# A hybrid decoder trunk on one core: the low part of every second weight unit from an accumulating DMA

## The chip, the core and the metric

The kernel runs on one core of one Trainium2 chip. The metric is the device time of one execution in microseconds (us), the median of several runs; lower is better. TensorE (PE) does the matmuls and loads their stationary operand (PEld), VectorE (DVE), ScalarE (ACT) and GpSimd (POOL) do the elementwise work, and SyncE (SP), ACT and POOL can issue DMAs.

## The reference

Two layers over a sequence of 512 tokens and a width of 1024, everything in float32. Cut to what is computed:

```python
def hybrid_layer(x, ...):
    h = rmsnorm(x, norm_g)
    proj = h @ w_in                      # 1024 -> 9216 columns, split into the names below
    (rq, rk, rv, rz, sq, sk, sv, sz, cu, cz, ga, gb, gc) = split(proj)
    y_a = retention(rq, rk, rv, ...) * silu(rz)
    y_b = stick_breaking(sq, sk, sv, ...) * silu(sz)
    y_c = s5_ssm(cu, ..., w_glu, b_glu) * silu(cz)
    merged = sigmoid(ga) * (y_a @ proj_a) + sigmoid(gb) * (y_b @ proj_b) + sigmoid(gc) * (y_c @ proj_c)
    return x + merged @ w_out
```

Most of the arithmetic is the products with `w_in`, `w_glu`, `proj_a`, `proj_b`, `proj_c` and `w_out`.

## The kernel before

**Split products.** PE multiplies in float32r, a float32 operand that is rounded. To keep the precision, each operand of a large product is held as two float32r tiles: a high part (the rounded value) and a low part (the value minus its high part). The helper `three` then issues three matmuls for each block: high times high, high times low, low times high.

**Units.** The host cuts all large weights of a layer into 98 units of 128 x 1024 floats (512 KB), so there are 196 in all, in the order in which PE consumes them. The text `ORDER_TEXT` gives that order by item: `sk sq sv sz gb cu cz pb gc rq rk rv0 rv1 glu ga pc rz pa out0 out1`, with parts of some items interleaved. There are two kinds of items. A token-major item (`sk sq sv cu rq rk rv0 rv1 out0 out1`) takes four units at once. It goes through four token blocks ("pieces"), each of which reads all four units one after the other, and only after the fourth piece are the units free. A channel-major item takes one unit (or half a unit) per piece and frees it right after.

**Buffers.** Raw weights, high parts and low parts share one pool `wp` of 12 buffers. The class `Weights` runs it: `load` issues the DMA of a raw unit on SP, `make` turns the oldest raw unit into a pair (`wh` by an ACT copy, `wl` by a DVE subtraction), `take` hands a pair to PE, and `fill` makes up to four pairs ahead and keeps up to four raw units loaded. After the last piece of a token-major item `W.free` rises by four and `fill` makes the four units of the next item in one go; this is called a seam below. A buffer is reused as soon as the pool hands it out again, and the new writer waits for the last reader of the old tile: ACT's next `wh` for PE's last matmul on an old pair, a raw load for the DVE subtraction or the matmul that read the buffer before.

**Order.** Instructions stand on each engine in the order in which the program writes them. One main loop goes over the pieces; in each step come background generators that are due, then the piece's matmuls, then `W.fill()`. Background work (evacuations of a piece, normalisation, attention, retention chunks, the state space model) is written as generators that yield to later steps. Another background chain, which prepares coefficients on POOL and DVE, advances when counters of the estimated load of POOL and DVE are low enough; the counters are kept by the wrappers `TT`, `TS`, `STT`, `GT`, `GS` and `MM` (all recorded under line 197).

Names used below: `raw`, `wh`, `wl` are the three tiles of a unit; `mm` is the PSUM tile of a piece; `hh`, `hl` the halves of the normalised input; `mgh`, `mgl` those of the merged branches; `yah`, `yal` those of the retention branch. A matmul `mm<-wl,hh` has the low weights as moving operand (token-major), `mm<-hh,wl` as stationary operand (channel-major).

Of the kernel before, what the change touches and what calls it, by code (L numbers as in the profile page):

```python
# [10 lines left out]
F32 = mybir.dt.float32  # L11
F32R = mybir.dt.float32r
BF16 = mybir.dt.bfloat16
AF = mybir.ActivationFunctionType
ALU = mybir.AluOpType
PSUM = bass.MemoryType.PSUM

P = 128
# [168 lines left out]
def trunk(ctx: ExitStack, tc, x_in, w_in, par_in, bc_in, ng_in, cst_in, rope_in, out):  # L187
    nc = tc.nc
    load = {"V": 0.0, "G": 0.0, "T": 0.0}

    def counted(f, engine, each):


        def g(*a, **k):
            o = k["out"] if "out" in k else a[0]
            load[engine] += 0.07 * (engine != "T") + each * math.prod(o.shape[1:])
            return f(*a, **k)  # L197

        return g

    TT = counted(nc.vector.tensor_tensor, "V", 1.04e-3)
# [3 lines left out]
    ACT = nc.scalar.activation  # L205
# [3 lines left out]
    wp = ctx.enter_context(tc.tile_pool(name="wp", bufs=W_TILES))  # L209
# [31 lines left out]
    def C(n):  # L241
# [7 lines left out]
        out=negm, in_=negm, pattern=[[1, P]], base=0, channel_multiplier=-1, compare_op=ALU.is_ge, fill=0.0  # L249
# [45 lines left out]
    class Weights:  # L295
# [16 lines left out]
        def make(self):  # L312
            if not self.raw:
                self.load()
            raw = self.raw[0]
            wh = wp.tile([P, 1024], F32R, tag="w", name="wh")
            wl = wp.tile([P, 1024], F32R, tag="w", name="wl")
            ACT(wh, raw, AF.Copy)  # L318
            TT(out=wl, in0=raw, in1=wh.bitcast(F32), op=ALU.subtract)
            self.units.append((wh, wl))  # L320
            self.raw.pop(0)
            self.made += 1
# [1069 lines left out]
```

## Time and profile before

| | |
|---|---|
| median of 2 runs | 1311.69 us (1311.26 to 1312.12) |
| profiled execution | 1311.17 us, span 1309.5 us |
| PE busy | 1271.7 us, 97% |
| PEld busy | 1048.5 us, 80% |
| DVE busy | 855.6 us, 65% |
| ACT busy | 537.6 us, 41% |
| POOL busy | 382.5 us, 29% |
| mean granted clock of PE | 0.992 |

The span runs from the first to the last instruction of the profiled execution, and the time of that execution contains 1.7 us around it. Busy times are sums of instruction durations on an engine; they overlap with each other. A wait is an idle time of an engine that a semaphore ended, put down to the instruction that gave it. The granted clock is 1.00 at 2.4 GHz and 0.50 at 1.2 GHz.

### The profile page before, as it was taken

What the parts mean: (1) busy time and instruction counts of PE and PEld (TensorE: products, weight loads), DVE (VectorE), ACT (ScalarE), POOL (GpSimd) and SP (SyncE); (2) the same over time, 40 slices, a digit from 0 to 9 for tenths busy, and PEclk for the clock granted to TensorE, in tenths of its full rate; (3) what the DMA queues carried; (4) which work ended last, traced back from release to release, by engine and by line L of the source; (5) the groups of instructions that cost most, each with busy time, mean ns of one, the idle gap of its engine ahead of it and who ended that gap; (6) DMA issues with size and microseconds to landing.
All of it is one profiled execution on the core that took longest, in us unless ns stands there. A gap on an engine that the chain in (4) does not pass through costs nothing. (4 is left out here: it accounts for less than half of the span.)

```text
span 1309.5 us, 16640 instructions
## 1 busy us (share of the span) xinstructions
PE 1271.7 (97%) x6360; PEld 1048.5 (80%) x6360; DVE 855.6 (65%) x1189; ACT 537.6 (41%) x919; POOL 382.5 (29%) x452
## 2 busy tenths in 40 slices
PE   6989989999999999999999999899999999999998
PEld 5867768788887888888888877788888878888887
DVE  5997678776785438556365576789657844575542
ACT  5445534445343534332244445344534534423311
POOL 3340036638442012000042000584555311210000
PEclk9989989999999999999999999899999999999999
DMA  6232221222322322234433222122241232222342
GB/s 223 90 124 77 65 65 49 81 81 89 119 68 65 104 77 77 81 97 141 161 118 127 81 65 71 43 81 65 84 127 65 65 120 90 65 74 88 97 135 75
DMA packets 37375, 120.05 MB, mean 92 GB/s; under 512 B 4144, under 2 KB 4528, under 8 KB 37296
## 3 DMA queue, kind: packets, MB, share of 16 engines
q1 hardware_dynamic: 29664, 105.40, 25.2%
q10 hardware_dynamic: 7632, 13.59, 3.1%
q8 instruction: 50, 0.82, 0.3%
q14 instruction: 29, 0.24, 0.1%
HBM read 114.78 MB, written 4.19 MB: 91 GB/s over the span
## 5 line engine op out<-in xcount | busy, mean ns | idle before, releaser
L197 DVE TENSOR_TENSOR wl<-raw,wh 128x1024 fp32r<-128x1024 f32 x196 | 251.6, 1294 | 114.6 <-ACT wh L318 111.8
L197 PE MATMUL mm<-hh,wh 128*128 128x512 f32 x640 | 256.0, 400 | 0.0
L197 PE MATMUL mm<-hh,wl 128*128 128x512 f32 x640 | 251.2, 393 | 4.9 <-DVE wl L197 4.9
L197 PE MATMUL mm<-hl,wh 128*128 128x512 f32 x640 | 250.7, 392 | 0.0
L318 ACT ACTIVATE wh<-raw 128x1024 fp32r<-128x1024 f32 x196 | 205.8, 1057 | 86.7 <-PE mm L197 38.9
L197 PE MATMUL mm<-wh,hh 128*128 128x512 f32 x512 | 207.5, 405 | 0.9 <-ACT hh L421 0.9
L197 PE MATMUL mm<-wl,hh 128*128 128x512 f32 x512 | 202.6, 396 | 4.3 <-DVE wl L197 4.3
L197 PE MATMUL mm<-wh,hl 128*128 128x512 f32 x512 | 202.0, 395 | 0.0
L197 PEld LDWEIGHTS mm<-hh,wl 128*128 128x128 f32 x640 | 120.8, 189 | 32.2 <-DVE wl L197 6.3
L197 PEld LDWEIGHTS mm<-hh,wh 128*128 128x128 f32 x640 | 121.0, 189 | 25.1 <-issue 1.6
L197 PEld LDWEIGHTS mm<-hl,wh 128*128 128x128 f32 x640 | 121.0, 189 | 23.5
L197 PEld LDWEIGHTS mm<-wl,hh 128*128 128x128 f32 x512 | 104.5, 204 | 24.5 <-DVE wl L197 7.8
L197 PEld LDWEIGHTS mm<-wh,hh 128*128 128x128 f32 x512 | 104.5, 204 | 19.0 <-ACT hh L421 1.3
L197 PEld LDWEIGHTS mm<-wh,hl 128*128 128x128 f32 x512 | 104.2, 204 | 18.4 <-DVE hl L197 0.3
L1051 DVE TENSOR_TENSOR_SCAN kp<-kp,zero 128x511 f32<-128x511 f32 (+1 forms) x64 | 67.6, 1076 | 26.2 <-ACT kp L1047 26.1
L994 ACT ACTIVATE gate<-mm 128x512 f32<-128x512 f32 x48 | 28.6, 596 | 114.2 <-PE mm L197 114.2
L197 POOL TENSOR_SCALAR ms<-ss 128x8 f32<-128x8 f32 (+3 forms) x56 | 19.1, 341 | 181.5 <-DVE ss L824 100.6
L197 POOL TENSOR_TENSOR rs<-ms,mhalf 128x8 f32<-128x8 f32 (+3 forms) x56 | 64.6, 1154 | 4.7
L1033 POOL CAST qd<-qd 64x512 fp32r<-64x512 f32 x16 | 16.3, 1016 | 134.1 <-ACT qd L1028 133.7
L822 ACT ACTIVATE sq<-mm 128x512 f32<-128x512 f32 x32 | 19.0, 593 | 84.6 <-PE mm L197 84.5
L197 PE MATMUL mm<-wl,mgh 128*128 128x512 f32 x128 | 50.1, 391 | 0.2
L197 PE MATMUL mm<-wh,mgh 128*128 128x512 f32 x128 | 49.9, 390 | 0.0
(253 smaller groups left out, 2263.2 us busy)
## 6 DMA issues: line engine op xcount, KB each, us to landing
raw<-in_w SPq DMA_DIRECT2D x196, 512.0 KB, 3.5
x<-in_x SPq DMA_DIRECT2D x8, 256.0 KB, 7.3
rope<-in_rope ACTq DMA_DIRECT2D x8, 256.0 KB, 3.7
xh<-in_x ACTq DMA_DIRECT2D x8, 256.0 KB, 4.4
x<-xh ACTq DMA_DIRECT2D x8, 256.0 KB, 2.0
xh<-x ACTq DMA_DIRECT2D x8, 256.0 KB, 4.6
out<-xh ACTq DMA_DIRECT2D x8, 256.0 KB, 2.1
gB<-in_ng SPq DMA_DIRECT2D x2, 256.0 KB, 5.8
```

Of the source, the lines that this page charges most:

```text
L197: return f(*a, **k)
L318: ACT(wh, raw, AF.Copy)
L822: ACT(s2, ps, AF.Square)
L994: ACT(sg, ps, AF.Sigmoid)
L1033: nc.gpsimd.tensor_copy(out=qd[h][o, :], in_=qd[h][r, :])
L1051: nc.vector.tensor_tensor_scan(v, v, zero1.to_broadcast([P, n - 1]), 1.0, ALU.mult, ALU.add)
```

## The change

From unit 9 on, every second unit (9, 11, ..., 195; 94 of 196) gets its low part in another way. ACT writes the negated high part into a tile `wn` (a copy of the raw weights with scale -1, rounded like `wh`). Then POOL issues a DMA from `raw` to `wn` that adds to what is there, so that `wn` ends as raw minus high. The DVE subtraction of these units goes. The other units are made as before.

```diff
             raw = self.raw[0]
             wh = wp.tile([P, 1024], F32R, tag="w", name="wh")
-            wl = wp.tile([P, 1024], F32R, tag="w", name="wl")
             ACT(wh, raw, AF.Copy)
-            TT(out=wl, in0=raw, in1=wh.bitcast(F32), op=ALU.subtract)
+            if self.made % 2 and self.made > 7:
+
+                wn = wp.tile([P, 1024], F32R, tag="w", name="wn")
+                ACT(wn, raw, AF.Copy, scale=-1.0)
+                nc.gpsimd.dma_start(out=wn, in_=raw, accum_op=ALU.add)
+                wl = wn
+            else:
+                wl = wp.tile([P, 1024], F32R, tag="w", name="wl")
+                TT(out=wl, in0=raw, in1=wh.bitcast(F32), op=ALU.subtract)
             self.units.append((wh, wl))
             self.raw.pop(0)
             self.made += 1
```

All token-major items begin at an even unit, so in each of them the second and the fourth unit are of the new kind. Lines of the changed kernel behind this place have numbers higher by 7.

Three places in the order of instructions follow, all at the seam from `out1` of layer 0 to `sk` of layer 1 (units 98 to 101). The waits in brackets name semaphores: those of engines, DMAHW for DMAs that SP or ACT issue, DMASW for those that POOL issues.

ACT at that seam, before: four high parts (`wh`) in a row, then the store and the squares of the last block of `out1`.

```order
L421 ACTIVATE hh_82<-T4_5721 128x4x128 [waits PE_49]
L318 ACTIVATE wh_5755<-raw_5585 128x1024 [waits DMAHW4_49,PE_49]
L318 ACTIVATE wh_5761<-raw_5591 128x1024 [waits DMAHW5_49,PE_49]
L318 ACTIVATE wh_5767<-raw_5597 128x1024 [waits DMAHW6_49,DVE_49]
L318 ACTIVATE wh_5773<-raw_5603 128x1024 [waits DMAHW7_49,DVE_49]
L1264 DMA x1_87<-xh_5524 128x512 [waits DMAHW0_49,DVE_49]
L404 ACTIVATE xn_5781,ss_5607<-xh_5524 128x512
```

The same place on ACT in the changed kernel, with the negated copies (`wn`) of the second and the fourth unit.

```order
L428 ACTIVATE hh_82<-T4_5766 128x4x128 [waits PE_49]
L317 ACTIVATE wh_5800<-raw_5628 128x1024 [waits DMAHW4_49,PE_49]
L317 ACTIVATE wh_5806<-raw_5635 128x1024 [waits DMAHW5_49,PE_49]
L321 ACTIVATE wn_5808<-raw_5635 128x1024 [waits DMASW2_49,PE_49]
L317 ACTIVATE wh_5813<-raw_5641 128x1024 [waits DMAHW6_49,DVE_49]
L317 ACTIVATE wh_5819<-raw_5648 128x1024 [waits DMAHW0_49,DVE_49]
L321 ACTIVATE wn_5821<-raw_5648 128x1024 [waits DMASW5_49]
L1271 DMA x1_87<-xh_5567 128x512 [waits DMAHW7_49,DVE_49]
L411 ACTIVATE xn_5828,ss_5652<-xh_5567 128x512
```

The second negated copy waits for DMASW5, which is the accumulating DMA of the second unit, and the store and the squares stand behind it.

POOL at the same seam in the changed kernel: the two DMA issues stand between the statistics (`ss`, `ms`, `rs`) of the last two blocks of `out1`, which stood next to each other before.

```order
L197 TENSOR_TENSOR ss_5596<-ss_5596 128x1 [waits Activation_49]
L197 TENSOR_SCALAR ms_5756<-ss_5596 128x1 [waits Pool_49]
L197 TENSOR_TENSOR rs_5754<-ms_5756,mhalf_84 128x1 [waits Pool_49]
L322 DMA wn_5808<-raw_5635 128x1024 [waits DMASW2_49,DMAHW5_49,DVE_49,Activation_49]
L322 DMA wn_5821<-raw_5648 128x1024 [waits DMASW7_49,DMAHW0_49,DMASW5_49,Activation_49]
L197 TENSOR_TENSOR ss_5652<-ss_5652 128x1 [waits Activation_49]
L197 TENSOR_SCALAR ms_5832<-ss_5652 128x1 [waits DVE_49,Pool_49]
```

The second issue waits for the first one's landing too, through ACT and by a wait of its own; the statistics of the last block follow behind it.

## Rows read from the trace of the kernel before

**Rows 1.** The page, parts 1 and 2: busy time per engine, granted clock in 40 slices.
```profile
PE 1271.7 (97%) x6360; PEld 1048.5 (80%) x6360; DVE 855.6 (65%) x1189; ACT 537.6 (41%) x919; POOL 382.5 (29%) x452
...
PEclk9989989999999999999999999899999999999999
```

**Rows 2.** PE's own waits: instruction, releaser, us in total, times, longest.
```profile
PE wt L1068 <- DVE w L197: 13.5, 8, 3.1
PE mm L197 <- DVE wl L197: 9.2, 7, 3.3
```

**Rows 3.** Timeline at a pa unit of layer 1 (unit 181): start us, duration us.
```profile
1209.14 1.04 ACT L318 ACTIVATE wh<-raw 128x1024 fp32r<-128x1024 f32 x1
...
1223.94 0.39 PE L197 MATMUL mm<-yah,wl 128*128 128x512 f32 x1
```

**Rows 4.** Timeline at the seam to sk of layer 1 (units 98 to 101).
```profile
660.90 2.02 ACT L318 ACTIVATE wh<-raw 128x1024 fp32r<-128x1024 f32 x2
663.25 2.19 ACT L318 ACTIVATE wh<-raw 128x1024 fp32r<-128x1024 f32 x2 [0.33 <-DVE wl L197]
...
666.86 0.39 PE L197 MATMUL mm<-wl,hh 128*128 128x512 f32 x1
...
669.58 0.39 PE L197 MATMUL mm<-wl,hh 128*128 128x512 f32 x1
```

**Rows 5.** The page, part 5: busy us, mean ns of one, idle before.
```profile
L197 DVE TENSOR_TENSOR wl<-raw,wh 128x1024 fp32r<-128x1024 f32 x196 | 251.6, 1294 | 114.6 <-ACT wh L318 111.8
...
L318 ACT ACTIVATE wh<-raw 128x1024 fp32r<-128x1024 f32 x196 | 205.8, 1057 | 86.7 <-PE mm L197 38.9
```

**Rows 6.** The page, parts 3 and 6: the load queue, and the unit loads' landing.
```profile
q1 hardware_dynamic: 29664, 105.40, 25.2%
...
raw<-in_w SPq DMA_DIRECT2D x196, 512.0 KB, 3.5
```

**Rows 7.** POOL's short operations: the page's group, and timelines of POOL and DVE.
```profile
L197 POOL TENSOR_TENSOR rs<-ms,mhalf 128x8 f32<-128x8 f32 (+3 forms) x56 | 64.6, 1154 | 4.7
...
14.06 0.19 POOL L197 TENSOR_SCALAR ms<-ss 128x1 f32<-128x1 f32 x1
...
18.51 1.05 POOL L197 TENSOR_SCALAR ms<-ss 128x1 f32<-128x1 f32 x1
...
17.15 2.35 DVE L197 TENSOR_TENSOR wl<-raw,wh 128x1024 fp32r<-128x1024 f32 x2
```

**Rows 8.** The four unit loads between 655 and 672 us: from issue to landing.
```profile
DMA to landing us min/median/max: 3.5/5.2/5.4
```

**Rows 9.** Timelines at the seams to sv of layer 0 and out1 of layer 1.
```profile
61.17 1.06 ACT L318 ACTIVATE wh<-raw 128x1024 fp32r<-128x1024 f32 x1 [0.55 <-PE mm L197]
...
65.75 0.40 PE L197 MATMUL mm<-wl,hh 128*128 128x512 f32 x1
...
1281.02 2.96 ACT L318 ACTIVATE wh<-raw 128x1024 fp32r<-128x1024 f32 x3 [0.36 <-PE mm L197]
...
1285.29 0.39 PE L197 MATMUL mm<-wl,mgh 128*128 128x512 f32 x1
```

**Rows 10.** Timelines at the fourth unit of out0 and the fourth of rq, layer 0.
```profile
621.70 1.04 ACT L318 ACTIVATE wh<-raw 128x1024 fp32r<-128x1024 f32 x1
...
624.06 0.50 PE L197 MATMUL mm<-wl,mgh 128*128 128x512 f32 x1
...
330.73 1.06 ACT L318 ACTIVATE wh<-raw 128x1024 fp32r<-128x1024 f32 x1 [0.27 <-ACT gate L994]
...
336.51 0.39 PE L197 MATMUL mm<-wl,hh 128*128 128x512 f32 x1
```

**Rows 11.** Busy time by stretch; behind POOL's come granted clock, DMA share and GB/s.
```profile
92.50:97.60 5.10, 5.10 (x12) 4.03 (x13) 3.94 (x4) 4.58 (x6) 0.85 (x2) 0.50 0.07 6
188.40:193.20 4.80, 4.80 (x16) 4.24 (x17) 4.61 (x5) 0.98 (x2) 1.26 (x2) 0.50 0.23 67
410.00:417.00 7.00, 6.44 (x29) 5.03 (x30) 5.65 (x5) 2.64 (x5) 1.00 (x1) 1.00 0.38 119
```

## The prediction

> **What bounds the kernel now.** The page's busy line and its clock line come first: TensorE (PE) is busy 1271.7 of 1309.5 us and the granted clock stands near full speed throughout [rows 1]. The list of PE's own waits comes next. Only two entries matter after the start: 13.5 us in 8 waits of the attention transposes for VectorE (DVE), and 9.2 us in 7 waits of projection matmuls for a low part that DVE had not finished [rows 2]. So a change that only relieves DVE can win at most 13.5 + 9.2 = 22.7 us, and a few microseconds of clock. A change that makes a weight half arrive later is paid by PE in full as soon as the lead is used up. The question is therefore how much lead the low parts have, and where.
>
> The lead is read unit by unit, from the end of a unit's high-part copy on ScalarE (ACT) to the first matmul that reads its low part. Where units are consumed one at a time (the channel-major items) it is long, as with the 13.8 us of a pa unit in layer 1 (1223.94 - 1210.18) [rows 3]. Where one token-major item follows another it is short. In the sk item of layer 1, the high parts of the four units run at 660.90 and 663.25 in two pairs. PE reads the second unit's low part at 666.86 and the fourth's at 669.58 [rows 4]. Four units occupy eight of the twelve buffers, so no new half can be written before the last block of the group before has read the old one. That leaves a fixed lead of a few microseconds at each such seam.
>
> **What the change removes and adds.** 94 of 196 units are touched (9, 11, ..., 195). DVE loses 94 x 1.294 = 122 us, ACT gains 94 negated copies of 1.057 us = 99 us [rows 5]; both engines stay well under PE's 1271.7 [rows 1]. GpSimd (POOL) gains 94 DMA issues. On throughput nothing here binds. Latency is what moves: an odd unit's low part was ready about 1.3 us after its high part. Now it takes a second ACT pass (1.06 with the handover 1.1), and then D, the time from the end of that pass to the landing of the accumulating transfer.
>
> D has no row, since no DMA is issued from POOL and none accumulates. I build it from the nearest rows. The load queue's packets took 25.2% of 16 engines' span for 105.40 MB, so 0.252 x 1309.5 / 105.40 x 0.524 = 1.64 us for one 512 KB unit, while such a load lands 3.5 us after its issue [rows 6]: 1.86 us are fixed. An accumulation must read two operands, 2 x 1.64 = 3.28 us. For the issue I take POOL's short power operation, 1.15 us [rows 7]. Finally the seams are where loads bunch: four loads land there after 5.2 us in the median against 3.5 over all [rows 6, 8]; half of that difference is 0.8. D = 1.15 + 1.86 + 3.28 + 0.8 = 7.1, taken as 7. From below: a plain load plus that contention, 3.5 + 0.8 = 4.3. From above: issue, two whole loads and the full contention, 1.15 + 7.0 + 1.7 = 9.8. I take 7 because two reads over the same engines is the nearest thing to what the transfer does.
>
> The Trainium skill, DMA: Bandwidth & Descriptors, section "Anatomy of one DMA — SWDGE (gpsimd) path", gives for a GpSimd-issued copy about 2.0 us plus its bytes at 436 GB/s, which is 3.2 us for this size. No run here shows one. By that price of a copy the sum below would be 25 us and the result 1337, a fifth of my cost; the skill's page prices a copy there and not an accumulation.
>
> **The two transfers of a group are in series.** This is the second half of the cost and it is not in the diff. The pool hands the buffer of the second unit's raw weights to the fourth unit's negated copy, so that copy waits for the second unit's transfer to land (the order of ACT shows the wait on a DMA of POOL). ACT stands meanwhile, and POOL's second issue stands behind it. So the second unit's low part lands 1.1 + D after its high part, and the fourth's 1.1 + D after that: 2.2 + 2D. PE needs the fourth's 2.73 us after the second's (669.58 - 666.86) [rows 4]. With a for the lead of the second unit, a seam costs 2.2 + 2D - 2.73 - a = 2D - 0.53 - a.
>
> The seams between token-major items with touched units are twelve: sv, rk, rv0, rv1, out1 in layer 0, and sk, sq, sv, rk, rv0, rv1, out1 in layer 1. Their a, in that order, are 3.5, 7.0, 4.2, 5.3, 3.0, 3.9, 3.5, 3.5, 7.0, 4.2, 5.3, 3.2, in sum 53.6; the first is 65.75 - 62.23, the last 1285.29 - 1282.08 [rows 9], and the one of sk 666.86 - 662.92 [rows 4]. At D = 7: 12 x 13.47 - 53.6 = 108.0 us.
>
> Two more places are short. The fourth unit of out0 is copied late, from 621.70, and read at 624.06, 1.3 us after that copy ends: 1.1 + 7 - 1.3 = 6.8, in two layers 13.6. The fourth of rq has 336.51 - 331.79 = 4.7: 3.4, in two layers 6.8 [rows 10]. Everywhere else I cost the change at nothing, because leads like that of pa cover 1.1 + D = 8.1. The tightest of the rest, the second unit of glu, has about that much and is left out; the second unit of out0 follows if D passes 7. Two queues move too. SP's raw loads now wait for landings before they reuse a buffer, but a group's loads are wanted a whole item later; without that cover a seam would wait one load, 3.5 us, more. On POOL the statistics of the last block stand behind the second issue, that is up to 2.2 + D late; their readers are PE transposes one or two pieces on, and PE stands for about as long, so nothing is added while that holds.
>
> **The clock.** After the waits of 3.3 and 3.1 us [rows 2] the granted clock is 0.50, that is 1.2 GHz instead of 2.4, for the 5.1 and 4.8 us of work that follow; a stretch with only 0.56 us of idle PE kept 1.00 [rows 11]. Half speed over some 5 us costs 2.5 us. In a seam the second wait (1.1 + D - 2.73 = 5.4 us) is longer than those, so the work behind it pays 2.5; the low stretch behind the first wait mostly falls into the second. Twelve seams and the two out0 places: 14 x 2.5 = 35.
>
> **Sum.** 108.0 + 13.6 + 6.8 + 35 = 163. The DVE waits that might go I leave at nothing, since those at the seams belong to even units, which stay on DVE. From the profiled execution, 1311.17 us (1.7 around its span, 0.5 under the median of the runs): 1311.2 + 163.4 = 1475 us, 12% slower. The measurement tells about 2% (26 us) from no change.
>
> **Rivals.** *The transfer is hidden.* If the accumulation lands within about 2.5 us of the negated copy, seams cost 2D - 0.53 - a only where a is below 4.5, some 7 us in all, and out0 2 x 2.3, together 11; DVE's relief could then give back the 22.7 us of PE waits and the three low-clock stretches, 7.5 us. That ends at 1311 + 11 - 30 = 1292, not slower. It decides from D = 3.3 downward, where the cost is 27 us. Against it: the plain load of the same bytes takes 3.5 [rows 6]. Chance 0.05.
>
> *POOL cannot issue while DVE works.* POOL and DVE already get in each other's way: a POOL scaling of one column took 1.05 us beside DVE's low parts of 17.15 to 19.50, and 0.19 at 14.06 [rows 7]. At a seam DVE makes the even units' low parts just then. One such wait of 1.2 us per issue makes D = 8.2: seams 136.8, out0 16, rq 9, clock 35, in all 197 and 1508 us. Chance 0.15. The Trainium skill, SBUF — State Buffer, section "Who interferes with whom", tells of descriptor writing that starves behind DVE's two-port modes, but excepts an operation of two tensors such as this one; by that rule the wait would be absent and D stays 7. The lengthened scaling above agrees with its other half, that a two-input DVE operation holds up a POOL instruction that reads.
>
> *The accumulation runs far below copy rate.* At D = 12 the seams cost 228, out0 23.6, rq 16.8, clock 35: 303 us, 1615. No row speaks for or against it. Chance 0.15.
>
> *ACT's standing spreads.* While ACT waits for a transfer (D - 2 = 5 us) it does no evacuation. At seams PE stands too, but in the three groups per layer where channel-major items follow token-major ones PE works on; if three matmul banks do not cover it, or the attention steps beside it slip, six places lose up to 5 us more: 1475 + 30 = 1505. Chance 0.10.
>
> **How the numbers follow.** The forecast, D between 4.3 and 9.8, has 0.55. Its ends: D = 4.3 gives 43.2 + 8.2 + 1.3 = 53 us, with second waits of 2.7 us that may leave the clock alone, 1364; D = 9.8 gives 175 + 19 + 12 + 35 = 242, 1553. The second and fourth rivals lie inside; that makes 0.80 and leaves out the hidden transfer and the very slow one. Faster by over 2% would need more than the 30 us that can be won at all, 0.01; within 2% the rest of the first rival, 0.04; slower 0.95.
>
> **What would show it.** Landing of the POOL transfers some 7 us after the negated copy; PE waits at the second and fourth unit of each seam, about 3.6 and 5.4 us, put down to the DMA; ACT idle before each fourth negated copy for about 5 us; clock 0.50 behind the longer waits; channel-major stretches unchanged in length. Wrong would be: landings under 3.3 us, no wait at the fourth unit apart from the second's, or a loss that lies in the channel-major stretches instead.

## The result and the profile after

The changed kernel takes 1466.86 us (median of 2 runs, 1464.35 to 1469.37) against 1311.69 us (1311.26 to 1312.12): a ratio of 1.1185, 95% interval 1.1151 to 1.1218. The forecast was 1475 us, in a range of 1364 to 1553.

The page of the changed kernel, parts 1, 2, 3, 5 and 6 (busy time, granted clock by slice, queues, groups, DMA issues):

```profile
PE 1323.8 (90%) x6360; PEld 1078.8 (74%) x6360; DVE 720.9 (49%) x1095; ACT 626.8 (43%) x1013; POOL 437.2 (30%) x546
...
PEclk9999999999999999999889999999999999999999
...
q1 hardware_dynamic: 29664, 105.40, 23.6%
q0 software_dynamic: 13536, 49.29, 17.5%
...
L322 POOL DMA_DIRECT2D wn<-raw x94 | 82.5, 878 | 721.6 <-ACT wn L321 679.3
...
wn<-raw POOLq DMA_DIRECT2D x94, 512.0 KB, 4.8
```

Against [rows 1] DVE is 135 us less busy and ACT 89 us more (122 and 99 were worked out from the single instructions). PE is busy 52.1 us longer with the same 6360 matmuls. That is half clock: the mean granted clock falls from 0.992 to 0.954, spread so thinly over the slices that the clock line of the page hides it. The transfers have a queue of their own (q0), and the median one lands 4.8 us after its issue.

PE's own waits in the changed kernel, to be read beside [rows 2]:

```profile
PE mm L197 <- DMA wn<-raw: 88.4, 29, 7.0
PE pk L197 <- POOL b L772: 15.6, 6, 5.3
PE mm L197 <- ACT rv L1174: 9.2, 2, 4.8
PE wt L1075 <- DVE w L197: 8.7, 10, 2.9
...
PE sbo L197 <- ACT wt L1081: 5.5, 2, 2.9
...
PE mm L197 <- DVE wl L197: 1.2, 1, 1.2
```

These nearly close the account of the span, which grew by 158.2 us (1467.7 - 1309.5). The waits for transfers are 88.4. Three new waits for POOL and ACT, which stand in no row of before, are 15.6 + 9.2 + 5.5 = 30.3. PE's busy time adds 1323.8 - 1271.7 = 52.1. The two waits for DVE give back 13.5 - 8.7 and 9.2 - 1.2, together 12.8. The sum is 88.4 + 30.3 + 52.1 - 12.8 = 158.0.

The timeline of the changed kernel at the seam to sk of layer 1, the place of [rows 4] (start us, duration us, engine, idle time before with its releaser):

```profile
730.81 2.00 ACT L317 ACTIVATE wh<-raw 128x1024 fp32r<-128x1024 f32 x2
732.87 1.06 ACT L321 ACTIVATE wn<-raw 128x1024 fp32r<-128x1024 f32 x1
...
734.23 0.91 POOL L322 DMA_DIRECT2D wn<-raw  x1 [3.10 <-ACT wn L321]
...
743.26 1.06 ACT L321 ACTIVATE wn<-raw 128x1024 fp32r<-128x1024 f32 x1 [6.03 <-DMA wn<-raw]
...
743.28 0.80 PE L197 MATMUL mm<-wn,hh 128*128 128x512 f32 x1 [6.38 <-DMA wn<-raw]
...
744.62 0.86 POOL L322 DMA_DIRECT2D wn<-raw  x1 [9.48 <-ACT wn L321]
...
752.71 0.79 PE L197 MATMUL mm<-wn,hh 128*128 128x512 f32 x1 [4.89 <-DMA wn<-raw]
```

This is the series of the prediction. The first transfer releases PE and ACT at the same time, ACT makes the fourth unit's negated copy, and the second transfer starts 10.4 us after the first. PE stands twice. The matmul after each wait takes 0.80 us instead of 0.39, and the granted clock (the number after POOL's) is 0.50 for the 3.1 us behind the first wait:

```profile
743.30:746.40 3.10, 3.10 (x7) 2.47 (x8) 0.95 (x2) 2.60 (x5) 1.61 (x4) 0.50 0.71 161
```

In the second wait this seam is the extreme and not the rule. Over the twelve seams PE's first waits sum to 56.8 us, 4.7 each, and the second ones to 14.9, of which 4.9 are here; with out0 (10.3), rq (4.1) and cu (2.3) they make up the 88.4.

The landings of these two, and of the second transfer of the next seam (to sq), which meets no other load, from the view of one tile in three windows:

```profile
DMA to landing us min/median/max: 8.1/8.5/9.0
...
DMA to landing us min/median/max: 8.3/8.3/8.3
...
DMA to landing us min/median/max: 4.4/4.4/4.4
```

The middle row is the first transfer of the seam to sq. A transfer alone takes 4.4 us. The first of a seam, beside two or three raw loads of the next group, takes 8.3 to 9.0 at seven seams and 5.5 to 7.1 at the four to rv0 and rv1; at out1 of layer 1, where no load is left, it takes 4.4. Over the twelve seams D, from the end of the negated copy to the landing, is 7.9 us in the mean for the first and 5.0 for the second.

### The profile page after: what moved, and what is told of

It is laid out like the page before. It is cut to its first block, busy times and chain, and to the rows that moved or that the text cites. A ratio compares the mean times of both kernels' runs of the same rounds, so it can differ in the third digit from the quotient of the medians.

```text
span 1467.7 us, 16893 instructions
## 1 busy us (share of the span) xinstructions
PE 1323.8 (90%) x6360; PEld 1078.8 (74%) x6360; DVE 720.9 (49%) x1095; ACT 626.8 (43%) x1013; POOL 437.2 (30%) x546
## 5 line engine op out<-in xcount | busy, mean ns | idle before, releaser
L322 POOL DMA_DIRECT2D wn<-raw x94 | 82.5, 878 | 721.6 <-ACT wn L321 679.3
L197 DVE TENSOR_TENSOR wl<-raw,wh 128x1024 fp32r<-128x1024 f32 x102 | 129.5, 1273 | 170.6 <-ACT wh L317 98.4
L197 PE MATMUL mm<-wn,hh 128*128 128x512 f32 x224 | 97.0, 433 | 68.6 <-DMA wn<-raw 68.6
L321 ACT ACTIVATE wn<-raw 128x1024 fp32r<-128x1024 f32 x94 | 98.8, 1051 | 82.7 <-DMA wn<-raw 79.5
L197 PE MATMUL mm<-hh,wl 128*128 128x512 f32 x320 | 126.6, 396 | 1.2 <-DVE wl L197 1.2
L197 PE MATMUL mm<-hh,wn 128*128 128x512 f32 x320 | 124.9, 390 | 0.0
L197 PE MATMUL mm<-wl,hh 128*128 128x512 f32 x288 | 117.5, 408 | 0.1
L197 PEld LDWEIGHTS mm<-wn,hh 128*128 128x128 f32 x224 | 49.0, 219 | 87.5 <-DMA wn<-raw 79.8
L197 PEld LDWEIGHTS mm<-hh,wl 128*128 128x128 f32 x320 | 61.0, 191 | 14.9 <-DVE wl L197 1.7
L197 PEld LDWEIGHTS mm<-hh,wn 128*128 128x128 f32 x320 | 60.1, 188 | 12.9
```

The costliest lines, as they stand in the source:

```text
L321: ACT(wn, raw, AF.Copy, scale=-1.0)
L322: nc.gpsimd.dma_start(out=wn, in_=raw, accum_op=ALU.add)
```

## The experiments

The theory: the transfer's latency D, doubled by the series of two in a group, makes PE stand, and half clock follows. The rivals: ACT's or DVE's changed work costs or gains something by itself; the loss lies in the channel-major stretches as well; D is long because of the load on the DMA engines, or because of the transfer itself.

### Where the loss lies: e4, e1, e2

**e4_no_transfer**

```diff
-                nc.gpsimd.dma_start(out=wn, in_=raw, accum_op=ALU.add)
```

> The changed kernel without the transfer: the negated high part is used as low part, so the addition of the raw weights is left out. ACT's extra pass stays. Theory: low parts are ready 1.1 us after the high part, as early as before, so no wait at the seams, and DVE's relief shows alone: 1285 to 1312 us. Rival (the extra ACT pass is a good part of the loss): above 1350 us.

It took 1311.0 us (one run; before, in the same job: 1310.65). PE's waits of this kernel:

```profile
PE wt L1074 <- DVE w L197: 14.9, 10, 3.1
PE T L404 <- DVE xn L197: 9.0, 2, 7.4
PE mm L197 <- DVE wl L197: 5.5, 6, 1.6
PE z L197 <- DVE ks L197: 4.3, 1, 4.3
PE mm L197 <- ACT hh L427: 0.8, 1, 0.8
```

ACT's 94 extra passes cost nothing. The relief of DVE takes 3.7 us from the wait for low parts, and 1.4 come back in the waits of `wt` and 3.5 in that of `z` (0.8 before). The list is whole: without the 94 subtractions and without the transfers PE waits neither for POOL nor for `rv`. The whole loss is the transfer's, with its issue on POOL.

**e1_channel_only** and **e2_token_only** (`UNIT_TOKEN` is 1 to 4 for the units of a token-major group, 0 for the others)

```diff
-            if self.made % 2 and self.made > 7:
+            if self.made % 2 and self.made > 7 and not UNIT_TOKEN[self.made]:   # e1; e2 without "not"
```

> The accumulating DMA is kept for the 58 odd units of channel-major items alone; the 36 odd units of token-major items get their low part from DVE again. Theory (the loss is the late arrival of low parts at the seams between token-major items): no wait of PE for an accumulating DMA is left, and what remains is the delay on POOL and ACT, at most 30 us, less some 10 us of DVE waits: 1300 to 1335 us, say 1315. Rival (every converted unit costs the same, by ACT, POOL or DMA throughput): 58/94 of the loss of 155 us stays, 1407 us.

> The complement: the accumulating DMA only for the 36 odd units of token-major items. Theory: the 88 us of PE waits for these transfers and the low clock behind them (some 45 us) stay, the delays of attention and state space model on POOL and ACT go: 1435 to 1455 us. Rival (same cost for each unit): 36/94 of 155 us, 1371 us.

e1 took 1354.57 us (1353.37 to 1356.38), a ratio of 1.034 (1.0323 to 1.0357): 44 us for units that the prediction had put down as free. e2 took 1417.21 (one run), 106 us over before. Both miss the ranges expected of them, e1 above its own and e2 below, and both lie nearer to these than to their rivals. The two add up to 150, nearly all of the loss. PE's waits in e1:

```profile
PE pk L203 <- POOL b L777: 14.2, 4, 4.6
...
PE mm L203 <- ACT rv L1179: 8.8, 2, 4.5
PE sbo L203 <- ACT wt L1086: 5.8, 2, 3.2
```

PE waits for no transfer here. It waits for POOL and for ACT, 28.8 us, and pays 16.0 us of busy time on top (1287.7). The timeline of e1 in the stretch behind cu of layer 0 shows why for `pk` and `sbo`:

```profile
219.92 0.86 POOL L327 DMA_DIRECT2D wn<-raw  x1 [6.29 <-ACT wn L326]
...
228.66 1.06 ACT L326 ACTIVATE wn<-raw 128x1024 fp32r<-128x1024 f32 x1 [5.56 <-DMA wn<-raw]
...
230.01 0.86 POOL L327 DMA_DIRECT2D wn<-raw  x1 [9.23 <-ACT wn L326]
...
230.25 0.62 ACT L1086 ACTIVATE wt<-wt 128x512 f32<-128x512 f32 x1
...
230.94 1.05 POOL L203 TENSOR_TENSOR ab<-bbr,y_re 128x512 f32<-128x512 f32 x1
```

The same series, away from token-major items: the negated copy of unit 31 takes the buffer that the transfer of unit 29 still reads. ACT stands 5.56 us, and behind it stand the copies of attention (wt). POOL stands 6.29 and 9.23 us in front of its issues, and behind them stands the preparation of coefficients (ab). That began at 230.94, while POOL had been free since about 213.6; PE waits 4.6 us, until 251.57, for the coefficients `b` that POOL makes behind it. The waits for `rv` arise in the same way behind rv1: ACT stands 5.67 us before the negated copy of unit 63, at 453.91, and the evacuation of `rv` follows at 454.87.

### What makes D: e3, e5, e6, e9, e11, e12

**e3_load_last**: a group's four pairs are made before the next raw loads are issued, so the fourth negated copy gets another buffer.

```diff
                 self.make()
-                self.load()
             self.load()
```

> The changed kernel with the raw loads of a seam issued after all four pairs instead of between them. Then the fourth unit's negated copy no longer takes the buffer of the second unit's raw weights, so the two transfers are not in series, and the loads start later than the first transfer. Theory: the landing of the first transfer falls from 8.5 us to 5 to 6, a seam costs 1.1 + D - a plus about 0.5, some 2 to 3 us instead of 8, and the low clock behind it mostly goes: 1340 to 1390 us, say 1365. Rival (the latency of one transfer makes the loss and the order of the loads does not matter): above 1430 us.

1409.71 us (1407.39 to 1412.03), a ratio of 1.0756 (1.0729 to 1.0783): 57 us of the loss gone, less than expected. ACT's waits for a transfer are gone, and with them PE's for rv and for the copies of attention. But in the view of the tile at the seam to sk of layer 1, the two transfers, now 2.8 us apart, land after 7.8 and 9.3 us:

```profile
DMA to landing us min/median/max: 7.8/8.5/9.3
```

And PE's waits for transfers, by the list of waits, have shrunk by 20 us only:

```profile
PE mm L197 <- DMA wn<-raw: 68.5, 23, 5.9
```

**e5_plain_copy**: without the accumulation.

```diff
-                nc.gpsimd.dma_start(out=wn, in_=raw, accum_op=ALU.add)
+                nc.gpsimd.dma_start(out=wn, in_=raw)
```

> The change with a plain copy from the raw tile in place of the accumulation (left out: the addition, so the low part becomes the raw weights). It prices the accumulation against a copy of the same bytes. If the second read counts, as my D had it (2 x 1.64 us in place of 1.64), an undisturbed transfer falls from 4.4 us to about 2.8 and the time to some 1400 us: twelve seams lose about 2 x 1.6 us less each, 38 in all, and out0 and the clock some 25 more. If the accumulation rides on the transfer at no cost, landings stay at 4.4 us alone and 5.5 to 9 at seams, and the time stays at 1467 within 10 us.

1403.98 us (one run). The page's queue:

```profile
q0 software_dynamic: 13536, 49.29, 9.9%
```

The landing of an undisturbed copy (fourth unit of sq, layer 1), from the view of the tile:

```profile
DMA to landing us min/median/max: 2.8/2.8/2.8
```

The second operand is real work. An accumulating transfer lands after 4.4 us where a copy lands after 2.8, and it occupies the 16 engines for 0.175 x 1467.7 / 94 = 2.73 us where the copy takes 0.099 x 1402.2 / 94 = 1.48. Of the loss, 63 us hang on that, by this one run.

**e6_one_per_group**: the fourth unit of a group goes back to DVE.

```diff
-            if self.made % 2 and self.made > 7:
+            if self.made % 2 and self.made > 7 and UNIT_TOKEN[self.made] != 4:
```

> The change without the fourth unit of each token-major group (76 transfers in place of 94; those fourth units go back to the DVE subtraction). The prediction's series gave the second wait of a seam 5.4 us and the half clock behind it 2.5: twelve seams, two places of out0 and two of rq would give back 65 + 35 + 17, some 1350 us. By the trace of the change the fourth unit's waits at seams sum to only some 13 us, with 10 at out0 and 4 at rq, since the first wait and the half clock behind it already cover most of the second transfer: then about 27 us plus a few of clock come back, 1430 to 1440 us, and the second unit's waits stay at some 5 to 6 us each at the seams.

1439.78 us (one run): only 27 us come back. The first transfer of a seam is now the only one. The view of the tile has it at sk of layer 1:

```profile
DMA to landing us min/median/max: 8.9/8.9/8.9
```

So it is not the second transfer that stretches it, and no other transfer of GpSimd is in flight; what runs beside it is three raw loads. The second unit's wait stays, in the list of PE's waits, with nearly 5 us each:

```profile
PE mm L203 <- DMA wn<-raw: 58.2, 12, 6.7
```

**e9_load_later**: e3, and no raw loads at all in a step that makes three or more pairs.

```diff
+            n = 0
             while self.made < min(self.free + W_BUFS, L * NU) and self.room(2):
                 self.make()
-                self.load()
-            self.load()
+                n += 1
+            if n < 3:
+                self.load()
```

> The change with the loads last, and with no raw loads at all in a step that makes three or more pairs: they go out a step later, so that the accumulating transfers of a seam meet no raw loads. With loads last alone it was 1410 us, with landings of 7.8 and 9.3 us at the seam to sk of layer 1. If the raw loads on the shared DMA engines stretch the transfers, landings fall to about 4.4 for the first and 5 to 6 for the second, PE's waits for transfers from 68 to some 25 us, and the time to 1350 to 1370. If the two transfers stretch each other, or GpSimd's queue sets the pace, landings stay at 7 to 9 and the time at 1400 to 1410.

1412.79 us (1410.65 to 1417.48), as e3. It did not do what it was meant to. The timeline of SP has the loads at the seam to sk all the same, just behind the first transfer's issue at 707.75:

```profile
708.18 7.58 SPq L308 DMA_DIRECT2D raw<-in_w  x3
```

The landings there, by the view of the tile, are those of e3:

```profile
DMA to landing us min/median/max: 7.7/8.5/9.4
```

SP has nothing else in its order here: a load goes out as soon as its buffer is free, wherever the program writes it. So the run says nothing on the loads.

**e11_load_after** and its control **e12_before_load_after**: after a token-major group the loads wait for two more steps and are issued by ACT, behind its evacuations (`self.skip` begins at -1; e12: the same in the kernel before).

```diff
-                nc.sync.dma_start(out=raw, in_=w_in[u // NU, u % NU])
+                eng = nc.scalar if self.skip == 0 else nc.sync
+                eng.dma_start(out=raw, in_=w_in[u // NU, u % NU])
...
+            if n > 2 and UNIT_TOKEN[self.made - 1] == 4:
+                self.skip = 2
+            elif self.skip > 0:
+                self.skip -= 1
+            else:
+                self.load()
+                self.skip = -1
```

> The change with the raw loads of a token-major group held back for real: ACT issues them behind the evacuations of the second block of the next item, some 13 us after the seam. Moving the loads later in the program did nothing (1413 us against 1410), since SP issues a load as soon as its buffer is free and the loads still ran at the seams. If the raw loads stretch the transfers of a seam, the first lands in some 4.4 to 5.5 us instead of 5.6 to 9.2, the second, which still overlaps with it, in 5 to 7 instead of 6.8 to 10, PE's waits for transfers fall from 67 to some 30 to 40 us, and the time to 1360 to 1380. If it is not the loads (the two transfers themselves, or GpSimd's queue), landings stay and the time stays at 1405 to 1415.

> The kernel before with the same held-back loads, as a control: they are wanted only some 13 us later, so 1311 us within 5. If it is slower, the difference is the price of the held-back loads and is taken off the run beside it.

e11 took 1380.43 us (1376.84 to 1381.59), a ratio of 1.0528 (1.0511 to 1.0545). In its timeline the loads of the seam to sk, whose first transfer is issued at 694.79, come 20 us later, from ACT:

```profile
715.38 1.41 ACTq L316 DMA_DIRECT2D raw<-in_w  x3
```

In the view of the tile at that seam, and at the seam to out1 of layer 0:

```profile
DMA to landing us min/median/max: 4.4/5.7/7.0
...
DMA to landing us min/median/max: 4.4/4.6/4.8
```

The first transfer at sk lands after 4.4 us; the second takes 7.0, with four coefficient loads beside it. At out1, where only a store of 256 KB runs beside them, the two take 4.4 and 4.8. PE's waits for transfers, from the list:

```profile
PE mm L203 <- DMA wn<-raw: 44.1, 20, 5.1
```

Over the twelve seams D is 4.9 us in the mean for the first transfer and 5.3 for the second, where e3, with the same distance of 2.8 us between the two, had 7.1 and 8.7. So two transfers 2.8 us apart hardly stretch each other, and the raw loads stretch them, at sk from 7.8 and 9.0 us (e3 and the change) to 4.4 without them. The control took 1316.9 (one run), 6 us more than before and just outside what was expected, with one new wait of 8.1 us (PE's `z` for POOL's `qd`, L1048); e11 has that wait too, 5.7 us long. With the transfers undisturbed, a seam still costs PE a wait at the second unit, because 4.7 us of D and 1.1 of the second pass are more than ten of the twelve leads of the prediction.

### What is left of the idea: e8, e13, e7

**e8_channel_load_last** is e1 with the loads last, as in e3. **e13_channel_without_coef** leaves out eight units per layer more:

```diff
-            if self.made % 2 and self.made > 7 and not UNIT_TOKEN[self.made]:
+            if self.made % 2 and self.made > 7 and not UNIT_TOKEN[self.made] and not 28 < self.made % NU < 44:
```

> Transfers for the 58 channel-major units alone, and a group's four pairs made before the next raw loads are issued. Made alone on 58 units the change cost 44 us, of which PE's waits were 14.2 for POOL's coefficients, 8.8 for ACT's evacuation of rv, 5.8 for ACT's copies in attention and the rest clock. Theory: ACT stood there 5.6 us at two places per layer because the negated copy of a unit took the buffer that the transfer of the unit before was still reading; with the loads last it does not stand, the waits for rv and for the copies vanish, and POOL's issue comes sooner: 1325 to 1340 us. Rival: POOL is simply late from the work of its issues (58 x 0.9 us) and DVE's sharing, and ACT's waits come from the extra passes: then 1350 to 1360 as before.

> The channel-major units alone with the loads last (1325 us, PE's waits for POOL's coefficients 13.5 us in 4), without the eight units per layer that lie between cu and rq, where POOL prepares the coefficients. If POOL is late because its issues stand in its order and wait for ACT's negated copy (5.9 and 2.0 us of standing at units 29 and 31), these four waits vanish with the half clock behind them: 1325 - 13.5 - 4 x 1.7 = 1305 to 1312 us, level with the kernel before. If the coefficients are late because the removed subtractions move the order in which they are prepared, the waits stay, and the time stays above 1320.

> The kernel before with the loads last, a control for the 1306.5 us of the 42 units that lie away from token-major items and coefficients. If the gain of 4 us over the kernel before is that of the loads' order alone, this comes to 1306 to 1308 us; if it comes from the subtractions that DVE no longer does (the removed wait of 3.3 us at a low part and the half clock behind it), this stays at 1310 to 1312.

e8 took 1325.24 us (1324.37 to 1326.85), a ratio of 1.0113 (1.0096 to 1.013): ACT's standing was worth 29 us of the 44. Its remaining new wait, in the list of PE's waits:

```profile
PE pk L203 <- POOL b L776: 13.5, 4, 4.2
```

POOL in the same stretch as above, in the timeline of e8:

```profile
217.40 0.86 POOL L327 DMA_DIRECT2D wn<-raw  x1 [5.85 <-ACT wn L326]
220.24 0.87 POOL L327 DMA_DIRECT2D wn<-raw  x1 [1.98 <-ACT wn L326]
```

e13 took 1306.53 us (1305.8 to 1307.61), a ratio of 0.9967 (0.9955 to 0.9978). The waits for coefficients are gone. By itself this does not tell POOL's standing from the removed subtractions, since e13 gives the eight units their subtractions back as well. e4 does: there all 94 subtractions are gone, and PE has no wait for POOL. So it was POOL's issues, and its standing in front of them, that made the coefficients late. Of the versions with the transfer e13 is the only one ahead of the kernel before, by 4.4 us. The control **e7_before_load_last**, the kernel before with the loads last, took 1310.09 (ratio 0.9991, 0.9982 to 1.0), so some 3.5 of the 4.4 us belong to the 42 units: PE's wait for a low part of 3.3 us [rows 2] is down to 1.6 at most, 2.0 us less over all waits for low parts, and PE is busy 2.7 us less than in e7 (1272.0 to 1269.3). Waits of PE in e13, which has 0.4 us for transfers:

```profile
PE mm L203 <- DVE wl L203: 7.2, 7, 1.6
...
PE mm L203 <- DMA wn<-raw: 0.4, 2, 0.2
```

## Why the prediction came out right

The total was off by 8 us, and that is in part luck: two errors of opposite sign nearly cancel. For the token-major places it had forecast all of the 163 us; e2 measured 106. For the channel-major units it had nothing; e1 measured 44. The prediction had itself named a loss in the channel-major stretches as a sign that it would be wrong, and in that part it was.

**The mechanism** held for the larger part: latency and not throughput, the seams, the series through the pool's buffers, ACT and POOL standing, PE's waits at the seams [rows 4, 9], half clock behind them [rows 11]. Of the two waits per seam the sizes came out the other way round: about 3.6 and 5.4 us were forecast, 4.7 and 1.2 were measured in the mean.

**D = 7** was right in the mean and wrong in its parts. The mean over the 24 transfers of the twelve seams is (7.9 + 5.0) / 2 = 6.5. The prediction had 6.3 us for issue, fixed part and two reads, and 0.8 for contention. The runs show 4.4 us plus 0.3 of handover for the first three, and up to 4.6 us for contention (D is 9.3 at sk). Counting two reads was right: e5 puts the second at 1.6 us, as the 1.64 worked out from [rows 6]. Issue and fixed part were too dear: 1.15 + 1.86 = 3.0 us, where the copy of e5 leaves 2.8 + 0.3 - 1.6 = 1.5 for them. The contention was too cheap, because [rows 8] showed loads among loads; there was no row of another kind of transfer among them.

**The seams** were to cost 108.0 us of waits. With the measured D the same formula gives 12 x (12.9 - 0.5) - 53.6 = 95, and PE waited 71.8. The rest was counted twice. The half-clock stretch behind the first wait lies inside the second transfer's time, as the prediction said. But what PE does there at half speed takes longer than the 2.73 us to the fourth unit, and shortens the second wait by as much; that was not taken off. At sk PE works for 4.5 us between its two waits (743.28 to 747.82), at other seams for 3.0 to 5.5. Over the eleven seams with a second wait this is 22 us more than 2.73 each, nearly all of the 23 between 95 and 71.8; it appears in PE's busy time instead. e6 agrees: without the second transfer only 27 us came back, not the 117 that its expectation had by the series. **out0 and rq** were to cost 13.6 + 6.8; PE waited 10.3 + 4.1. **The clock** was to cost 35 us; PE's busy time grew by 52.1 in all, and by 33.4 in e2, which has the places that the 35 was for.

**"Everywhere else I cost the change at nothing"** was the step that failed. The leads do cover the low parts, and PE waits for no transfer in e1. But ACT and POOL are in order, and what stands behind a waiting copy or issue is not covered by the lead of a low part. The prediction had seen this for ACT, as a rival of 0.10 priced at 30 us. e8 against e1 puts it at 29, on top of the forecast and not in its place. For POOL it had looked at the statistics alone, and there it was right: PE's transposes `T`, which read what is scaled by them, wait 8.4 us in the changed kernel and 9.0 before. It missed the coefficients, which the change puts behind issues that wait for ACT: 13.5 us of waits, and 19 us in all by e13 against e8.

**DVE's relief** at nothing was right where nothing else changes (e4). In the changed kernel PE's waits for DVE shrank by 12.8 us. That PE now spends these elsewhere first is argued, not shown.

**The rivals.** The hidden transfer needed D under 3.3; even alone it is 4.7. POOL locked out by DVE is refuted: at the seam above the issue begins 0.3 us after the negated copy ends. The issues at 414.23 and 1150.70 (the second units of rv0) lie whole beside a low part that DVE makes, and they take 0.92 and 0.91 us where the mean of the 94 is 0.88; the wait of 1.2 us isn't there. The rule of the Trainium skill cited there (SBUF — State Buffer, "Who interferes with whom") agrees with these two issues. The price of a copy that the prediction took from the Trainium skill (DMA: Bandwidth & Descriptors, "Anatomy of one DMA — SWDGE (gpsimd) path"), 3.2 us, is near the 2.8 that e5 shows for an undisturbed copy. e5 still took 1404 us and not the 1337 that the sum gave for such a transfer: beside the raw loads its D is 6.3 us in the mean for the first transfer of a seam, and PE waits 28.1 us for coefficients, `rv` and attention copies, nearly as long as in the changed kernel (30.3). (The 25 us of that sum are under a sixth of the 163, not a fifth.) The accumulation far below copy rate did not come: it runs at about the copy's rate on twice the bytes.

## What to carry to other kernels

A step that moves from an engine to a DMA is priced by its latency among the transfers that run at that moment, so look at what the seam itself triggers: here the loads of the next group nearly doubled it at most seams. Then list what stands behind each new wait on every in-order engine, and the one that issues the DMA above all; those costs come on top of the wait on the critical path. Use such a transfer only where the lead is long and the issuing engine has nothing due: 42 of the 94 units did that here, with the loads issued last, and gained 4 us (0.3%) where all 94 lost 155.

## What the runs showed of the hardware

- An accumulating transfer of 512 KB within SBUF takes 4.4 us alone from the start of its issue to landing, a plain copy 2.8. It costs the DMA engines 2.73 us against 1.48, and GpSimd 0.88 us against 0.57.
- Beside three 512 KB loads it takes 9.0 us at sk of layer 1, though the DMA engines' mean busy share is only 0.75 there, and beside four loads of coefficients and a store, 256 KB each, 8.1 us at a share of 0.83. The windows of these two transfers (busy us of PE, PEld, DVE, ACT, POOL, then granted clock, DMA share, GB/s):

```profile
734.20:743.30 9.10, 2.72 (x17) 2.02 (x15) 3.15 (x4) 1.78 (x3) 0.91 (x1) 0.81 0.75 182
744.60:752.70 8.10, 3.22 (x10) 2.19 (x9) 1.29 (x2) 1.30 (x4) 6.14 (x8) 0.71 0.83 205
```

- One load is enough, and its distance counts. At rz:0 and rz:4 of both layers a single raw load, issued some 0.3 us behind the transfer, leaves it 7.0 to 8.0 us; at gb:1 and gb:6, where the load is issued 2.7 us behind, it lands after 4.5. The load and the landing at rz:0 of layer 0 (transfer issued at 559.25), then at gb:1 of layer 0 (135.14):

```profile
559.56 0.33 SPq L308 DMA_DIRECT2D raw<-in_w  x1
...
DMA to landing us min/median/max: 8.0/8.0/8.0
...
137.81 0.33 SPq L308 DMA_DIRECT2D raw<-in_w  x1
...
DMA to landing us min/median/max: 4.5/4.5/4.5
```

- Two accumulating transfers 2.8 us apart hardly delay each other (4.4 and 4.8 us in e11). A load 2.7 us behind hardly does either, so no run here shows that a load is worse than a second transfer; that a load's packets stand between the transfer's on the same engines is argued, not shown.
